# The hi/lo split of streamed weights, 1024 columns at a time instead of 512

## The chip, the cores and the metric

One core of one Trainium2 chip. The metric is the device time of one execution in microseconds (us); the kernel before was executed three times for it. A further execution was recorded by the hardware profiler, and all rows below come from that one.

## The reference, cut to what matters

Two small networks of float32 run one after the other on 512 tokens of width 1024.

```python
def first_block(x, ...):                     # DEPTH = 2
    for layer in range(2):
        h = rms_norm(x, norm_mix[layer])
        if layer < 1:
            x = x + short_conv_mixer(h, a_w_in, a_conv_w, a_w_out)
        else:
            x = x + nsa_mixer(h, b_w_qg, b_w_o, shared, rel_bias)   # three attention branches
        x = x + squared_relu_mlp(rms_norm(x, norm_mlp[layer]), mlp_w1[layer], mlp_w2[layer])
        if layer == 0:
            shared = nsa_shared_kv(rms_norm(x, kv_norm), w_kv, ...)  # with compress_blocks (phi)
    return rms_norm(x, final_norm)
# then, with 16 meta tokens set in front: mixer_block (z, xbc, dt, q, k, v and two gates from one
# product u @ w_in; an SSD scan in blocks of 128, a sliding-window attention with a sink, merged and
# projected), conv_ffn (d_ff 2816), a last norm
```

Nearly all the arithmetic is `activations @ weights`. Each weight is used once, for all 512 or 528 tokens, so the kernel streams 362 blocks ("chunks") of 128 x 1024 float32 weights, 512 KB each, in the order of their use.

## The kernel before, in words

**Three products for one.** The result has to be as exact as float32, and TensorE is fed with a rounded float32 type, `fp32r`. So each weight `w` is split: `whi` is `w` rounded to `fp32r` (a copy on ScalarE, ACT, line 161), `wlo = w - whi` (a subtraction, line 163, on VectorE, DVE, or on GpSimd, POOL). The activations have the same two parts, `hh` and `hl`, and a product is three matmuls: high by high, high by low, low by high.

**The stream.** `Stream` owns the weights. A chunk comes by one DMA on SyncE's queue (SP) into a tile `w32` of 1024 columns, of which there are two. It is split in two halves of 512 columns, into `whi` and `wlo`, of which there are four each, so four halves. A half holds four slots of 128 columns; `take` hands out the next slot, or two of them. At the first slot of a half `pre(half)` runs: it issues DMAs up to chunk `half // 2 + 1` and splits up to half `half + 2`. Half h goes into the buffers that half h - 4 had, so its split waits until TensorE (PE) has done the last matmul on that one. Halves are numbered 0 to 723, chunks 0 to 361; half h belongs to chunk h // 2. With `begin`, the first chunk is loaded in two pieces.

**Which engine subtracts.** `lo_mod` decides: a half with `ns % 4 < lo_mod` goes to POOL, the others to DVE. It is LO1 = 2 in the `nsa` stage (halves of every second chunk), LO2 = 4 in the window attention and the SSD stage (all halves), 0 elsewhere.

**Scaled splits.** Halves 192 to 209 and 226 to 249 are weights that are multiplied by a norm's gain while they are split. They are in the table `plan`; each is split in two or four pieces by pairs of instructions, ACT in line 157 and DVE in line 158, both with a scale.

**The order.** The kernel is written with the Tile framework, which orders each engine's instructions when the kernel is built, on a clock of its own: of those that it holds to be ready, the earlier in the program goes first. On the chip each engine then runs its own list in order, and a waiting instruction holds those behind it. All the weight DMAs are on SP's list, beside SP's loads of biases and its spills.

**The stages, in order of time.** `layer_a` (a convolution mixer); from about 90 to 143 us 48 DMAs on POOL's queue also write the skewed bias tables (`biases`). Then `mlp` 0, dense: matmul upon matmul of 512 columns. `nsa`: `kvraw` makes raw keys and values `kr`; `ebuild(s)` adds position terms to them, 32 additions `e` of which DVE runs 24 in a row (line 676); `kvsteps(0)` makes the first keys and values from scaled weights, its second half of the weights being chunk 104 (halves 208 and 209); `phi(s)` multiplies 8 chunks in all by `e`, two slots at a time, between steps of the attention; `br_a` and `br_b` are attention steps whose minima (of negated scores) and exponentials run on DVE (line 844) and ACT (line 846). `mlp` 1. Then the second network: `swa` (window attention; `head` has lines 1173 to 1224, and between the heads `xbc` and `gate_unit` run, with lines 1277 and 1283), `ssd` (the scan), `merge`, `ffn`, `tail`. In `swa` and `ssd` products are made by `gemm2`, which takes the 8 slots of a whole chunk first and then goes over them twice, once for each half of the 528 tokens.

`mm` in the rows is line 257, through which all matmuls go; line 266 is the low part of `split`, which splits activations.

Of the kernel before, what the change touches and what calls it, by code (L numbers as in the profile page):

```python
# [10 lines left out]
F32 = mybir.dt.float32  # L11
F32R = mybir.dt.float32r
I32 = mybir.dt.int32
AF = mybir.ActivationFunctionType
ALU = mybir.AluOpType
# [4 lines left out]
P = 128  # L20
# [23 lines left out]
BK = (2, 2, 2, 2)  # L44
PB = 10
PPB = 9


def _bucket(d):
# [73 lines left out]
class Stream:  # L123
# [9 lines left out]
    def begin(self, cols):  # L133
        c0, c1 = cols
        if c0 == 0:
            self.w32[self.nd] = self.pool.tile([P, 1024], F32, tag="w32", name="w32", bufs=2)
            self.nd += 1
        self.b.nc.sync.dma_start(self.w32[self.nd - 1][:, c0:c1], self.src[self.nd - 1][:, c0:c1])

    def pre(self, half):  # L140
        b, nc = self.b, self.b.nc
        while self.nd < min(self.nch, half // 2 + 2):
            t = self.pool.tile([P, 1024], F32, tag="w32", name="w32", bufs=2)
            nc.sync.dma_start(t, self.src[self.nd])
            self.w32[self.nd] = t
            self.nd += 1
        while self.ns < min(2 * self.nch, half + 3):
            c, o = divmod(self.ns, 2)
            src = self.w32[c][:, o * 512:o * 512 + 512]
            h = self.pool.tile([P, 512], F32R, tag="whi", name="whi", bufs=4)  # L150
            l = self.pool.tile([P, 512], F32R, tag="wlo", name="wlo", bufs=4)
            if self.ns in self.plan:
                g, ks = self.plan[self.ns]
                n = 512 // len(ks)
                for i, k in enumerate(ks):
                    a, sc = slice(i * n, i * n + n), b.pv(g, k)
                    nc.scalar.activation(out=h[:, a], in_=src[:, a], func=AF.Copy, scale=sc)
                    nc.vector.scalar_tensor_tensor(out=l[:, a], in0=src[:, a], scalar=sc, in1=h[:, a].bitcast(F32),  # L158
                                                   op0=ALU.mult, op1=ALU.subtract)
            else:  # L160
                nc.scalar.activation(out=h, in_=src, func=AF.Copy)  # L161
                eng = nc.gpsimd if self.ns % 4 < self.lo_mod else nc.vector
                eng.tensor_tensor(out=l, in0=src, in1=h.bitcast(F32), op=ALU.subtract)  # L163
            self.hl[self.ns] = (h, l)
            if o:
                del self.w32[c]
            self.ns += 1

    def take(self, key, r0, c0, n=128, width=1, rows=128):
        half, j = divmod(self.pos, 4)  # L170
        if j == 0:
            self.pre(half)
            self.hl.pop(half - 1, None)
        assert j + width <= 4
        for w in range(width):
            self.order.append((key, r0, c0 if isinstance(c0, tuple) else c0 + 128 * w, n))
        self.pos += width
        h, l = self.hl[half]
        a = j * 128
        e = a + (n if width == 1 else 128 * width)  # L180
        return h[:, a:e], l[:, a:e]


class Builder:
# [391 lines left out]
    def nsa(self, c):  # L576
# [87 lines left out]
        def ebuild(s):  # L664
            for b in range(2):
                for jh in range(2):
# [5 lines left out]
                    for g in range(4):  # L672
                        rr = slice(64 * (g % 2), 64 * (g % 2) + 64)
                        src = raws[s][g // 2][rr, A].rearrange("p (n j q) -> p q j n", j=8, q=2)
                        for q in range(2):
# [4 lines left out]
                                op=ALU.add)  # L680
                    eh, el = til("pp", PPB, "eh", F32R), til("pp", PPB, "el", F32R)
                    self.split(eh, el, e)
# [176 lines left out]
        def br_b(h, b, dst):  # L859
# [5 lines left out]
            for kts in ((0,), (1,), (2, 3)):  # L865
# [3 lines left out]
                for kt in kts:  # L869
                    segs.append((kt, off))  # L870
                    for qb in range(kt, 4):
                        self.tr(pt[:, off:off + 128], dst[qb][:, kt * 128:kt * 128 + 128])
                        off += 128
                ph, pl = til("pp", PPB, "ph", F32R), til("pp", PPB, "pl", F32R)
                self.split(ph[:, 0:off], pl[:, 0:off], pt[:, 0:off])
# [953 lines left out]
```

## Time and profile before

| What | Value |
|---|---|
| median of 3 runs | 2491.11 us (2489.51 to 2494.75) |
| the profiled execution, first to last instruction (span) | 2492.6 us |
| PE (TensorE matmul), busy | 2399.2 us, 96% |
| DVE (VectorE), busy | 1621.5 us, 65% |
| ACT (ScalarE), busy | 1116.3 us, 45% |
| POOL (GpSimd), busy | 596.3 us, 24% |
| mean granted clock of TensorE | 0.983 of full speed |
| DMA, mean | 97 GB/s |

A share of busy time is a mean over stages that have different limits; the rows by stretch below are the better guide. PEld is TensorE's loading of weights, which lies beside its matmuls. In a row `out<-in` names the tiles written and read, with partitions x elements and type; `x` stands ahead of a count; behind the bar is the idle time of the engine just ahead of these instructions, and what ended it. [...]

### The profile page before, as it was taken

How to read it: one execution, taken by the hardware profiler on the slowest of the kernel's cores; microseconds unless marked ns; L12 is line 12 of the kernel's file. 1: busy time of each engine (PE TensorE's matmuls, PEld its weight loads, DVE VectorE, ACT ScalarE, POOL GpSimd, SP SyncE). 2: the span in 40 equal slices, each digit the busy share in tenths (PEclk: the TensorE clock that was granted, in tenths of full speed). 3: DMA queues.
4: the chain of work that ended last, by engine and by line, in shares of the span. 5: the costliest groups of instructions: out<-in, count | busy, mean ns of one | idle time of the engine just before them, and what ended most of it. 6: DMA issues, size and time to landing. Idle time of an engine off the chain costs nothing.

```text
span 2492.6 us, 37785 instructions
## 1 busy us (share of the span) xinstructions
PE 2399.2 (96%) x14273; PEld 2090.8 (84%) x14273; DVE 1621.5 (65%) x3220; ACT 1116.3 (45%) x2252; POOL 596.3 (24%) x597
## 2 busy tenths in 40 slices
PE   8999999998899989999999989998999999999997
PEld 6778888886787768888888889988889999998996
DVE  6456525548888776435458894688987565874774
ACT  4233323333777663223435765555555433442442
POOL 1210000002434430000135445466656201000001
PEclk9999999999999999999999999999999999999998
DMA  4763333332421332322333222321212452333222
GB/s 144 175 155 92 97 93 93 102 117 83 130 86 51 103 93 93 94 93 93 95 99 108 67 75 90 94 65 52 64 52 85 145 188 91 95 90 95 90 93 77
DMA packets 87219, 242.68 MB, mean 97 GB/s; under 512 B 15435, under 2 KB 21835, under 8 KB 86987
## 3 DMA queue, kind: packets, MB, share of 16 engines
q1 hardware_dynamic: 82768, 228.96, 29.6%
q0 software_dynamic: 3136, 10.04, 2.0%
q8 instruction: 112, 1.84, 0.3%
q10 hardware_dynamic: 1132, 1.26, 0.2%
q14 instruction: 71, 0.58, 0.1%
HBM read 223.18 MB, written 24.51 MB: 99 GB/s over the span
## 4 chain that ended last, share of the span: by engine, by line
PE 82%; DVE 12%; ACT 2%; issue 2%; DMA 1%; SPq 0%; POOL 0%; DVEq 0%; ACTq 0%; POOLq 0%
PE mm L257 71%; PE o L257 3%; PE g L257 3%; PE s L257 2%; DVE cvt L1283 2%; PE pt L261 1%; DMA w<-in_ws_dram 1%; DVE pl L266 1%; PE u L257 1%; PE u L261 1%; DVE pp L1173 1%; PE st L257 0%; ACT ph L265 0%; DVE e L676 0%; DVE q L1109 0%
## 5 line engine op out<-in xcount | busy, mean ns | idle before, releaser
L257 PE MATMUL mm<-hh,whi 128*128 128x258 f32 (+2 forms) x2464 | 801.4, 326 | 25.5 <-ACT hh L305 6.9
L257 PE MATMUL mm<-hh,wlo 128*128 128x258 f32 (+2 forms) x2464 | 801.8, 326 | 6.4 <-DVE wlo L158 6.4
L257 PE MATMUL mm<-hl,whi 128*128 128x258 f32 (+2 forms) x2464 | 800.2, 325 | 2.6 <-DVE hl L306 2.6
L161 ACT ACTIVATE whi<-w 128x512 fp32r<-128x512 f32 x682 | 427.7, 630 | 814.9 <-PE mm L257 656.7
L163 DVE TENSOR_TENSOR wlo<-w,whi 128x512 fp32r<-128x512 f32 x516 | 362.5, 704 | 336.8 <-ACT whi L161 323.2
L257 PEld LDWEIGHTS mm<-hh,whi 128*128 128x128 f32 x2464 | 467.2, 190 | 71.6 <-ACT hh L305 9.8
L257 PEld LDWEIGHTS mm<-hh,wlo 128*128 128x128 f32 x2464 | 468.0, 190 | 50.1 <-DVE wlo L158 6.8
L257 PEld LDWEIGHTS mm<-hl,whi 128*128 128x128 f32 x2464 | 468.0, 190 | 46.3 <-issue 4.5
L163 POOL TENSOR_TENSOR wlo<-w,whi 128x512 fp32r<-128x512 f32 x166 | 232.7, 1408 | 209.1 <-ACT whi L161 179.9
L257 PE MATMUL mm<-b,whi 128*128 128x512 f32 (+1 forms) x699 | 273.5, 391 | 0.0
L257 PE MATMUL mm<-a,wlo 128*128 128x512 f32 (+1 forms) x699 | 273.5, 391 | 0.0
L257 PE MATMUL mm<-a,whi 128*128 128x512 f32 (+1 forms) x699 | 273.0, 391 | 0.0
L257 PEld LDWEIGHTS mm<-a,wlo 128*128 128x128 f32 x699 | 131.7, 188 | 29.9
L257 PEld LDWEIGHTS mm<-b,whi 128*128 128x128 f32 x699 | 131.7, 188 | 29.8
L257 PEld LDWEIGHTS mm<-a,whi 128*128 128x128 f32 x699 | 131.7, 188 | 29.7
L257 PE MATMUL mm<-oh,whi 128*128 128x258 f32 (+1 forms) x400 | 123.1, 309 | 2.8 <-ACT oh L265 2.1
L257 PE MATMUL mm<-ol,whi 128*128 128x258 f32 (+1 forms) x400 | 123.5, 309 | 0.0
L257 PE MATMUL mm<-oh,wlo 128*128 128x258 f32 (+1 forms) x400 | 123.5, 309 | 0.0
L291 POOL TENSOR_TENSOR acc<-sq 128x512 f32<-128x512 f32 (+1 forms) x5 | 7.0, 1397 | 438.1 <-ACT sq L286 438.1
L533 DVE TENSOR_TENSOR u<-mm,rstd 128x512 f32<-128x512 f32 x64 | 44.2, 691 | 88.6 <-PE mm L257 84.0
L996 POOL TENSOR_TENSOR sq<-sq 128x512 f32<-128x512 f32 x6 | 8.1, 1346 | 336.5 <-ACT sq L990 336.5
L257 PEld LDWEIGHTS mm<-oh,whi 128*128 128x128 f32 x400 | 76.7, 192 | 9.0 <-ACT oh L265 2.7
(535 smaller groups left out, 4260.2 us busy)
## 6 DMA issues: line engine op xcount, KB each, us to landing
w<-in_ws_dram SPq DMA_DIRECT2D x361, 512.0 KB, 3.5
sk<-line POOLq DMA_DIRECT2D x16, 320.0 KB, 10.5
bias<-sk SPq DMA_DIRECT2D x16, 256.0 KB, 2.9
sk<-line POOLq DMA_DIRECT2D x16, 192.0 KB, 10.0
x<-xs SPq DMA_DIRECT2D x8, 264.0 KB, 3.0
tatt<-gu SPq DMA_DIRECT2D x8, 258.0 KB, 2.3
matt<-yat SPq DMA_DIRECT2D x8, 258.0 KB, 2.0
yacc<-ya SPq DMA_DIRECT2D x8, 258.0 KB, 2.0
```

Source lines behind the costliest of these rows:

```text
L161: nc.scalar.activation(out=h, in_=src, func=AF.Copy)
L163: eng.tensor_tensor(out=l, in0=src, in1=h.bitcast(F32), op=ALU.subtract)
L257: self.nc.tensor.matmul(out, l, r, start=start, stop=stop)
L261: self.nc.tensor.transpose(out, in_, self.ident[0:n, 0:n])
L266: (eng or nc.vector).tensor_tensor(out=lo, in0=src, in1=hi.bitcast(F32), op=ALU.subtract)
L291: (nc.vector if k >= 6 else nc.gpsimd).tensor_tensor(out=na[:, c0:c1], in0=acc[:, c0:c1], in1=sq[:, c0:c1], op=ALU.add)
L533: nc.vector.tensor_tensor(out=u[:, XS], in0=p, in1=r[:, XS], op=ALU.mult)
L996: eng.tensor_tensor(out=a1[:, XS], in0=a1[:, XS], in1=s1[:, XS], op=ALU.add)
L1173: nc.vector.tensor_tensor_reduce(out=pp[:, b, 0:n], in0=s[:, 0:n], in1=bb, scale=1.0, scalar=nsink[:, h:h + 1], op0=ALU.add, op1=ALU.min, ...
L1283: nc.vector.scalar_tensor_tensor(out=t[:, s:W], in0=u[:, 0:W - s], scalar=hw(k), in1=t[:, s:W], op0=ALU.mult, op1=ALU.add)
```

## The change

A chunk is now split as a whole. `whi` and `wlo` are tiles of 1024 columns, two of each (WS = 2) in place of four of 512, so they take the same room. One ACT copy and one subtraction do the 1024 columns. Chunk 0 and the chunks with halves in `plan` are still split in halves or pieces, with the same instructions as before, into the large tiles. `pre` runs once per chunk: at the first slot of chunk `ch` it issues DMAs up to chunk `ch + 2` and splits up to chunk `ch + 1`. Chunk c takes the buffers of chunk c - 2. `lo_mod` goes by the number of the chunk: a chunk goes to POOL as a whole or not at all, as before, for both values in use.

```diff
--- before.py
+++ after.py
@@ -44,6 +44,8 @@
 BK = (2, 2, 2, 2)
 PB = 10
 PPB = 9
+WD = 2
+WS = 2
 
 
 def _bucket(d):
@@ -133,49 +135,53 @@
     def begin(self, cols):
         c0, c1 = cols
         if c0 == 0:
-            self.w32[self.nd] = self.pool.tile([P, 1024], F32, tag="w32", name="w32", bufs=2)
+            self.w32[self.nd] = self.pool.tile([P, 1024], F32, tag="w32", name="w32", bufs=WD)
             self.nd += 1
         self.b.nc.sync.dma_start(self.w32[self.nd - 1][:, c0:c1], self.src[self.nd - 1][:, c0:c1])
 
-    def pre(self, half):
+    def pre(self, ch):
         b, nc = self.b, self.b.nc
-        while self.nd < min(self.nch, half // 2 + 2):
-            t = self.pool.tile([P, 1024], F32, tag="w32", name="w32", bufs=2)
+        while self.nd < min(self.nch, ch + WD + 1):
+            t = self.pool.tile([P, 1024], F32, tag="w32", name="w32", bufs=WD)
             nc.sync.dma_start(t, self.src[self.nd])
             self.w32[self.nd] = t
             self.nd += 1
-        while self.ns < min(2 * self.nch, half + 3):
-            c, o = divmod(self.ns, 2)
-            src = self.w32[c][:, o * 512:o * 512 + 512]
-            h = self.pool.tile([P, 512], F32R, tag="whi", name="whi", bufs=4)
-            l = self.pool.tile([P, 512], F32R, tag="wlo", name="wlo", bufs=4)
-            if self.ns in self.plan:
-                g, ks = self.plan[self.ns]
-                n = 512 // len(ks)
-                for i, k in enumerate(ks):
-                    a, sc = slice(i * n, i * n + n), b.pv(g, k)
-                    nc.scalar.activation(out=h[:, a], in_=src[:, a], func=AF.Copy, scale=sc)
-                    nc.vector.scalar_tensor_tensor(out=l[:, a], in0=src[:, a], scalar=sc, in1=h[:, a].bitcast(F32),
-                                                   op0=ALU.mult, op1=ALU.subtract)
+        while self.ns < min(self.nch, ch + WS):
+            c = self.ns
+            src = self.w32.pop(c)
+            h = self.pool.tile([P, 1024], F32R, tag="whi", name="whi", bufs=WS)
+            l = self.pool.tile([P, 1024], F32R, tag="wlo", name="wlo", bufs=WS)
+            halves = [(2 * c + o, slice(o * 512, o * 512 + 512)) for o in range(2)]
+            if c == 0 or any(i in self.plan for i, _ in halves):
+                for i, hs in halves:
+                    if i in self.plan:
+                        g, ks = self.plan[i]
+                        n = 512 // len(ks)
+                        for j, k in enumerate(ks):
+                            a, sc = slice(hs.start + j * n, hs.start + j * n + n), b.pv(g, k)
+                            nc.scalar.activation(out=h[:, a], in_=src[:, a], func=AF.Copy, scale=sc)
+                            nc.vector.scalar_tensor_tensor(out=l[:, a], in0=src[:, a], scalar=sc, in1=h[:, a].bitcast(F32),
+                                                           op0=ALU.mult, op1=ALU.subtract)
+                    else:
+                        nc.scalar.activation(out=h[:, hs], in_=src[:, hs], func=AF.Copy)
+                        nc.vector.tensor_tensor(out=l[:, hs], in0=src[:, hs], in1=h[:, hs].bitcast(F32), op=ALU.subtract)
             else:
                 nc.scalar.activation(out=h, in_=src, func=AF.Copy)
-                eng = nc.gpsimd if self.ns % 4 < self.lo_mod else nc.vector
+                eng = nc.gpsimd if 2 * c % 4 < self.lo_mod else nc.vector
                 eng.tensor_tensor(out=l, in0=src, in1=h.bitcast(F32), op=ALU.subtract)
-            self.hl[self.ns] = (h, l)
-            if o:
-                del self.w32[c]
+            self.hl[c] = (h, l)
             self.ns += 1
 
     def take(self, key, r0, c0, n=128, width=1, rows=128):
-        half, j = divmod(self.pos, 4)
+        ch, j = divmod(self.pos, 8)
         if j == 0:
-            self.pre(half)
-            self.hl.pop(half - 1, None)
-        assert j + width <= 4
+            self.pre(ch)
+            self.hl.pop(ch - 1, None)
+        assert j + width <= 8
         for w in range(width):
             self.order.append((key, r0, c0 if isinstance(c0, tuple) else c0 + 128 * w, n))
         self.pos += width
-        h, l = self.hl[half]
+        h, l = self.hl[ch]
         a = j * 128
         e = a + (n if width == 1 else 128 * width)
         return h[:, a:e], l[:, a:e]
```

## Rows read from the trace of the kernel before

**Rows 1.** The chain that ended last: shares of the span by engine.
```profile
PE 82%; DVE 12%; ACT 2%; issue 2%; DMA 1%; SPq 0%; POOL 0%; DVEq 0%; ACTq 0%; POOLq 0%
```

**Rows 2.** Busy time by stretch: stretch, length, PE PEld DVE ACT POOL, PEclk, DMA share, GB/s.
```profile
300.00:400.00 100.00, 100.00 (x432) 81.09 (x431) 33.44 (x50) 24.02 (x38) 0.00 (x0) 1.00 0.31 95
1330.00:1500.00 170.00, 153.97 (x1207) 146.06 (x1207) 149.79 (x371) 114.24 (x300) 78.43 (x84) 0.98 0.26 74
1680.00:1900.00 220.00, 205.14 (x1466) 188.83 (x1465) 189.97 (x336) 118.28 (x251) 133.39 (x92) 0.95 0.20 62
600.00:660.00 60.00, 47.10 (x251) 38.64 (x249) 50.42 (x119) 34.93 (x86) 26.83 (x38) 0.89 0.41 126
```

**Rows 3.** The chain of 1330 to 1500 us, then of 1680 to 1900 us, by line.
```profile
by line: DVE cvt L1283 9.3%; DVE pp L1173 8.9%; issue 8.1%; PE mm L257 7.8%; DVE pl L266 6.2%; DVE q L1109 4.2%; PE g L257 4.1%; DVE pm L1186 4.0%; DVE tm L1184 3.5%; DVE of L1224 3.5%; PE u L261 3.3%; ACT pp L1176 3.1%; PE s L257 2.7%; DVE
by line: PE mm L257 43.9%; DVE cvt L1283 10.8%; PE u L257 4.4%; PE o L257 4.4%; DVE Ml L266 3.7%; DVE xs L1542 3.2%; PE s L257 2.6%; PE u L261 2.5%; DVE u L1277 2.0%; DVE cl L266 1.6%; ACT L L1490 1.5%; DVE dl L360 1.5%; DVE y L1503 1.4%; i
```

**Rows 4.** What PE waits for: us in all, times, longest us.
```profile
PE mm L257 <- DVE wlo L158: 6.4, 1, 6.4
...
PE mm L257 <- ACT whi L161: 5.2, 3, 3.8
```

**Rows 5.** Groups of the page: count, busy us, mean ns, idle before and its releaser.
```profile
L161 ACT ACTIVATE whi<-w 128x512 fp32r<-128x512 f32 x682 | 427.7, 630 | 814.9 <-PE mm L257 656.7
L163 DVE TENSOR_TENSOR wlo<-w,whi 128x512 fp32r<-128x512 f32 x516 | 362.5, 704 | 336.8 <-ACT whi L161 323.2
...
L163 POOL TENSOR_TENSOR wlo<-w,whi 128x512 fp32r<-128x512 f32 x166 | 232.7, 1408 | 209.1 <-ACT whi L161 179.9
```

**Rows 6.** Groups of instructions by form, whole span: lengths of different widths.
```profile
L1190 POOL TENSOR_TENSOR pp<-pp,rc 128x768 f32<-128x768 f32 x16 | 23.6, 1475 | 0.0
L846 ACT ACTIVATE pa<-pa,mn 128x512 f32<-128x512 f32 x32 | 23.0, 719 | 12.2 <-DVE mn L844 11.9
L844 DVE CUSTOM_DVE_ANT_0 pa<-s,bias 128x512 f32<-128x512 f32 x32 | 21.9, 685 | 0.5 <-DMA bias<-sk 0.5
L846 ACT ACTIVATE pc<-pc,mn 128x256 f32<-128x256 f32 x32 | 16.1, 503 | 2.1 <-DVE mn L844 1.8
L844 DVE CUSTOM_DVE_ANT_0 pc<-s,bias 128x256 f32<-128x256 f32 x32 | 13.4, 418 | 5.1 <-PE s L257 4.9
...
L1188 POOL TENSOR_TENSOR pp<-pp,rc 128x128 f32<-128x128 f32 x16 | 6.5, 409 | 45.4 <-DVE rc L1181 33.9 <-ACT of L1223 7.4 <-DVE ms L372 4.2
```

**Rows 7.** Timeline of POOL, then of DVE, 1424 to 1430 us: start, us, instruction.
```profile
1425.63 1.28 POOL L163 TENSOR_TENSOR wlo<-w,whi 128x512 fp32r<-128x512 f32 x1
...
1425.67 1.80 DVE L1283 SCALAR_TENSOR_TENSOR cvt<-u,hw,cvt 128x527 f32<-128x527 f32 x1
...
1427.87 0.75 DVE L1283 SCALAR_TENSOR_TENSOR cvt<-u,hw,cvt 128x526 f32<-128x526 f32 x1
```

**Rows 8.** Timeline of ACT, 108 to 150 us; in brackets idle before, and its releaser.
```profile
140.32 1.15 ACT L161 ACTIVATE whi<-w 128x512 fp32r<-128x512 f32 x2 [8.76 <-DMA w<-in_ws_dram]
```

**Rows 9.** Timeline of DVE, 588 to 640 us.
```profile
607.61 0.88 DVE L158 SCALAR_TENSOR_TENSOR wlo<-w,pkt,whi 128x256 fp32r<-128x256 f32 x2
...
609.60 10.05 DVE L676 TENSOR_TENSOR e<-kr,pkt 64x128 f32<-64x128 f32 x24
...
619.68 0.88 DVE L158 SCALAR_TENSOR_TENSOR wlo<-w,pkt,whi 128x256 fp32r<-128x256 f32 x2
```

**Rows 10.** Timeline of PE, 612 to 625 us.
```profile
613.43 0.40 PE L257 MATMUL mm<-hl,whi 128*128 128x512 f32 x1
...
621.25 0.63 PE L257 MATMUL mm<-hh,whi 128*128 128x512 f32 x1
```

**Rows 11.** Timeline of PE, 634 to 640 us.
```profile
637.03 0.39 PE L257 MATMUL mm<-wlo,eh 128*128 128x256 f32 x1 [0.86 <-POOL wlo L163]
```

**Rows 12.** Groups of POOL, 1330 to 1500 us, then 1680 to 1900 us.
```profile
L163 POOL TENSOR_TENSOR wlo<-w,whi 128x512 fp32r<-128x512 f32 x33 | 43.8, 1336 | 27.7 <-ACT whi L161 20.0 <-ACT ph L265 5.2 <-PE s L257 2.3
L163 POOL TENSOR_TENSOR wlo<-w,whi 128x512 fp32r<-128x512 f32 x47 | 69.9, 1494 | 56.2 <-ACT whi L161 43.1 <-DVE cvt L1283 6.0 <-DVE y L1503 3.7
```

## The prediction

> **What bounds the kernel now.** I read the chain of waits first: PE holds 82% of it, DVE 12%, ACT 2% [rows 1]. Then the busy time by stretch [rows 2]: in the dense stages PE is busy 100 of 100 us and issues 432 matmuls, one per 0.2315 us, so nothing a split does there can shorten the time; it can only add, by coming too late. In the window attention (1330 to 1500 us) PE idles 16.0 of 170 us and DVE is busy 149.8; in the SSD stage (1680 to 1900 us) PE idles 14.9 of 220 us and DVE is busy 190.0. There DVE leads: the DVE lines that the chain of those stretches names add up to 39.6% and 24.2% of it [rows 3]. Last, the list of what PE waits for: 6.4 us in one piece for a low part of line 158 and 5.2 us for high parts [rows 4]. So I price the change by stage: does a split of 1024 columns still arrive, and what does it hold up while it runs?
>
> **How many, and how long.** The 682 copies of line 161 [rows 5] become 2 + 340 (chunk 0 stays in halves), the 516 DVE subtractions 2 + 257, the 166 POOL subtractions 83; the 88 scaled pairs of lines 157 and 158 stay. No instruction of 1024 columns is in the trace. On ACT 256 more columns cost 0.719 - 0.503 = 0.216 us [rows 6], so 1024 take 0.630 + 0.432 = 1.06 us (bounds: 0.63 and 1.26, twice a half). On DVE 0.685 - 0.418 = 0.267 us per 256 gives 0.704 + 0.534 = 1.24 us (0.70 to 1.41). On POOL 640 columns more cost 1.475 - 0.409 = 1.07 us [rows 6], which would make 1.41 + 0.85 = 2.26 us; twice a mean half is 2.82, and twice a half that meets nobody (1.28, [rows 7]) 2.56. I take 2.4. So a chunk saves ACT 0.20 us, DVE 0.17 us, POOL about 0.2 us of busy time.
>
> **Dense stages: nothing.** A half-split starts when PE leaves its buffer (of the 814.9 us that ACT is idle ahead of its copies, PE ends 656.7, [rows 5]) and is used three halves later. [...] The DMAs of w32 keep two buffers and wait for the same split as before; issued one chunk earlier in SP's program, they are moved past SP's bias loads and spills, at 0.
>
> **Bias skew, 90 to 143 us.** Here the weight DMAs are late; ACT splits the moment they land (8.76 us idle for the DMA before 140.32, [rows 8]). PE can now start on such a chunk only when all 1024 high columns are copied: 1.06 - 0.63 = 0.43 us later, and its first low part 0.43 + 0.53 = 0.96 us later. The lateness does not add up from chunk to chunk, since the DMAs set the pace. I take +0.8 us (0 to 2).
>
> **The queue of ebuild, 604 to 628 us.** Chunk 104 holds halves 208 and 209, the second half of the kvsteps(0) weights, both scaled splits. In the trace half 208's two subtractions ran at 607.61, before ebuild(1); half 209's stood behind 24 additions of 10.05 us and ran at 619.68 [rows 9]. [...] Half 208 got ahead because its buffer came free half a chunk before the raw keys were ready. After, chunk 104 waits for PE to leave all of chunk 102, which is the moment at which kr of ebuild(1) becomes ready too; among ready instructions the earlier in the program goes first, so all four subtractions now stand behind the 24 additions. PE then stops 12 matmuls earlier (2.8 us), resumes some 0.9 us earlier, as 208's subtractions no longer precede the additions, and has 20 matmuls left instead of 8. [...] I take +3.0. [...]
>
> **phi, 625 to 656 us.** Eight chunks are eaten between attention steps. PE already waited 0.86 us for a POOL half [rows 11]; the whole chunk's low part comes 2.4 - 1.28 + 0.43 = 1.5 us later. Most of it lies beside waits for the attention's minima. I take +0.8 us (0 to 3).
>
> **Port, 1330 to 1960 us.** All low parts are on POOL here. At 1425.63 POOL began a low part of 1.28 us; DVE's line 1283 began at 1425.67 and took 1.80 us, where the same line took 0.75 us at 1427.87 [rows 7]: DVE stood still until POOL had ended. So what counts is how long one POOL instruction holds DVE's queue. Before it meets the hold DVE works on for x us, and loses hold - x. With two halves, some microseconds apart, a chunk costs 2(1.28 - x), with one instruction 2.4 - x. The difference is x - 0.16. At x = 0 the change gains 0.16 us a chunk; at x = 1.28 (half-holds lost nothing) it costs 1.1. With DVE's operations 0.4 to 0.75 us long I take x = 0.6: +0.44 us a chunk. The two stretches have 33 and 47 halves [rows 12], 16.5 and 23.5 chunks, so 7.3 and 10.3 us of DVE time; of that I put one half and three tenths on the path [rows 3]: 3.6 + 3.1 = +6.7 us. The bounds become -2.5 and +17 us.
>
> [...]
>
> **What the savings give back.** 340 x 0.20 us of ACT and 257 x 0.17 us of DVE are mostly beside a busy PE; on the path the splits stand with 5.2 us of PE's waits [rows 4], most of it the DMA's. I take -1.0 us (0 to -5).
>
> **Sum.** 0 + 0.8 + 3.0 + 0.8 + 6.7 - 1.0 = +10.3 us. The profiled execution spans 2492.6 us, 1.5 over the median of the runs, 2491.11, and inside their 2489.5 to 2494.8; it would become 2502.9. On the median that is 2501.4 us, 0.41% slower.
>
> **Rivals.** (1) Not slower: the order of DVE's queue at 604 us turns the other way. Place and price: the four subtractions of chunk 104 stand before the additions, PE's 6.4 us wait goes, -9 instead of +3.0, sum -1.7, 2489.4 us. For it: in the trace 208 did get ahead. Against it: 209 did not, and it had the same release that the whole chunk has now. It decides as soon as the planner sees the chunk's high part ready before kr. (2) The long hold costs nothing, because DVE loses as much to two holds as to one (x near 0.16), or its lost time falls beside PE's work: +3.6, 2494.7 us. For it: PE is still busy 91% and 93% of the two stretches [rows 2]. Against it: the 1.05 us lost in [rows 7]. (3) Slower still, through ACT: its queue is in order, and a copy that starts only when PE has left the whole chunk holds the exponentials behind it 0.43 us longer: 40 chunks x 0.43 = 17 us in the two stretches, half of it on the path, +8.6 on top, 2510.0 us. For it: ACT's exponentials are links of the attention's chain. Against it: ACT is idle a third of the first stretch and nearly half of the second.
>
> **Chances.** Forecast 0.45 (own range 2496.5 to 2505), rival one 0.16, two 0.23, three 0.16. A measurement of this kernel tells about 0.2% (5 us) from no change. Slower by more: the forecast and rival three but for their edges, 0.57. Within: rival two and a part of rival one, 0.27. Faster: the rest of rival one and what a new order of instructions may bring, 0.16. The range reaches from 2486 to 2512 us.
>
> **What would show it.** Dense stages: PE still 100 of 100 us with 432 matmuls. ebuild: the scaled subtractions of one chunk together, before or after the 24 additions; PE's wait near 8.3 us if after. Bias skew: PE's waits for high parts 1 us longer in total. Port: POOL instructions of 2.3 to 2.6 us, DVE operations of 2.5 us and more beside them, DVE's busy time in the two stretches up by some 17 us, and PE's idle time there up by 5 to 8. I am wrong if PE starves in a dense stage, if the POOL instruction is much under 2.3 us, or if DVE's busy time in the two stretches does not rise.

## The result, and the profile after

The changed kernel takes 2520.35 us (median of 4 runs, 2519.18 to 2523.21) where the kernel before took 2492.08 in the same comparison: ratio 1.0118, 95% interval 1.0102 to 1.0134, some 28 us slower. The direction was the one forecast; the size was not, +10.3 us, and the range ended at 2512. The profiled execution spans 2519.0 us, 26.4 more than that of before.

The first question is in which stage the time went. Counting the weight matmuls from the start gives the moment at which each kernel is done with a given chunk. Chunk 133, the end of the `nsa` stage, ends 1.8 us later than before (935.9 and 937.7), chunk 197 2.3 us later (1296.2 and 1298.5), and chunk 288, with which the window attention, the SSD stage and the first products after them are done, 26.0 us later (2052.3 and 2078.3). From there on nothing is added: chunk 361 is 26.0 us late too. So one stretch has 24 us of the 26, and it is the one in which POOL does all low parts.

Busy time by stretch of the kernel before, from the end of chunk 197 to that of chunk 288 (columns: stretch, length, PE, PEld, DVE, ACT, POOL with their instructions, granted clock, DMA share, GB/s):

```profile
1296.00:2052.00 756.00, 721.88 (x5537) 685.15 (x5537) 582.95 (x1176) 402.19 (x888) 364.81 (x296) 0.98 0.29 91
```

The same view of the changed kernel, a dense stage ahead of it:

```profile
300.00:400.00 100.00, 100.00 (x432) 81.09 (x431) 31.39 (x32) 20.18 (x20) 0.00 (x0) 1.00 0.31 95
1298.00:2078.00 780.00, 727.74 (x5540) 687.90 (x5539) 614.96 (x1160) 387.91 (x797) 338.18 (x223) 0.97 0.28 87
```

The dense stage is what it was [rows 2]: 100 of 100 us, 432 matmuls. In the other stretch ACT and POOL have less to do, as the merging intends, and DVE, which lost 16 instructions, is busy 32 us longer. PE's idle time goes from 34.1 to 52.3 us; the other 6 us of the 24 are PE itself, busy 727.7 instead of 721.9 us at a granted clock of 0.97 instead of 0.98 (PEclk in [rows 2], a share of full speed).

The chain of waits of the changed kernel (one row; before: [rows 1]), then the groups that answer to [rows 5]:

```profile
PE 74%; DVE 15%; ACT 4%; DMA 3%; issue 2%; POOL 1%; SPq 0%; DVEq 0%; ACTq 0%; POOLq 0%
...
L169 ACT ACTIVATE whi<-w 128x1024 fp32r<-128x1024 f32 x340 | 359.9, 1059 | 870.7 <-PE mm L263 614.4
...
L171 DVE TENSOR_TENSOR wlo<-w,whi 128x1024 fp32r<-128x1024 f32 x257 | 315.2, 1227 | 229.2 <-ACT whi L169 229.1
...
L171 POOL TENSOR_TENSOR wlo<-w,whi 128x1024 fp32r<-128x1024 f32 x83 | 205.5, 2476 | 214.5 <-ACT whi L169 206.6
```

PE's share of the chain falls from 82% to 74%, DVE's rises from 12% to 15%, ACT's from 2% to 4%, DMA's from 1% to 3% and POOL's from 0% to 1%. DMA's part has grown mostly by loads between 2030 and 2071 us, a place where the changed kernel falls back by only 1 us more. The instructions themselves are as long as estimated: ACT 1.059 us (1.06), DVE 1.227 (1.24), POOL 2.476 (2.4).

What such a POOL instruction does to DVE shows in one place; the timeline of POOL in the changed kernel, 1430 to 1434 us, and then that of DVE:

```profile
1430.38 2.38 POOL L171 TENSOR_TENSOR wlo<-w,whi 128x1024 fp32r<-128x1024 f32 x1 [0.46 <-ACT whi L169]
```

```profile
1430.41 2.43 DVE L1190 TENSOR_TENSOR tm<-pp,rc 128x64 f32<-128x64 f32 x1
1432.76 0.42 DVE L1283 TENSOR_TENSOR u<-mm,rstd 128x264 f32<-128x264 f32 x1
1433.10 0.75 DVE L1289 SCALAR_TENSOR_TENSOR cvt<-u,hw,cvt 128x526 f32<-128x526 f32 x1
```

A DVE operation on 64 columns began 0.03 us after POOL's and took 2.43 us; it ended 0.08 us after POOL's. The next one, another operation and four times as wide, took 0.42.

Last, what PE waits for, of the weights' parts (us in all, times, longest; before: [rows 4]):

```profile
PE mm L263 <- DVE wlo L163: 6.9, 1, 6.9
...
PE mm L263 <- ACT whi L169: 2.9, 3, 1.8
PE mm L263 <- DVE wlo L171: 2.4, 4, 0.9
...
PE mm L263 <- POOL wlo L171: 1.4, 1, 1.4
```

Beside the one wait of 6.9 us, which is outside the stretch (its place is in the section on the prediction), PE hardly ever waits for a split. The 24 us don't come from splits that are late for PE, at least not directly.

### The profile page after: what moved, and what is told of

It is laid out like the page before. It is cut to its first block, busy times and chain, and to the rows that moved or that the text cites. A ratio compares the mean times of both kernels' runs of the same rounds, so it can differ in the third digit from the quotient of the medians.

```text
span 2519.0 us, 36649 instructions
## 1 busy us (share of the span) xinstructions
PE 2405.5 (95%) x14273; PEld 2090.9 (83%) x14273; DVE 1618.8 (64%) x2963; ACT 1050.6 (42%) x1912; POOL 571.4 (23%) x514
## 4 chain that ended last, share of the span: by engine, by line
PE 74%; DVE 15%; ACT 4%; DMA 3%; issue 2%; POOL 1%; SPq 0%; DVEq 0%; ACTq 0%; POOLq 0%
PE mm L263 64%; PE o L263 3%; PE g L263 2%; DVE cvt L1289 2%; PE s L263 2%; DMA w<-in_ws_dram 2%; PE pt L267 1%; ACT whi L169 1%; DMA ma<-matt 1%; DVE e L682 1%; PE u L267 1%; DVE pl L272 1%; DVE z L1529 1%; PE u L263 1%; DVE Ml L272 1%
## 5 line engine op out<-in xcount | busy, mean ns | idle before, releaser
L169 ACT ACTIVATE whi<-w 128x1024 fp32r<-128x1024 f32 x340 | 359.9, 1059 | 870.7 <-PE mm L263 614.4
L171 DVE TENSOR_TENSOR wlo<-w,whi 128x1024 fp32r<-128x1024 f32 x257 | 315.2, 1227 | 229.2 <-ACT whi L169 229.1
L171 POOL TENSOR_TENSOR wlo<-w,whi 128x1024 fp32r<-128x1024 f32 x83 | 205.5, 2476 | 214.5 <-ACT whi L169 206.6
L552 DVE TENSOR_TENSOR x<-mm,x 128x512 f32<-128x512 f32 x32 | 22.1, 692 | 110.7 <-PE mm L263 110.7
```

Source lines behind the costliest of these rows:

```text
L552: nc.vector.tensor_tensor(out=x[:, XS], in0=p, in1=x[:, XS], op=ALU.add)
```

## The experiments

Two theories stood at first. **Hold**: while POOL's subtraction runs, a DVE operation beside it stands still to its end, so the length of one POOL instruction sets what DVE loses. **Lead**: with whole-chunk buffers a split may start only when PE has left a whole chunk, so everything behind it comes later. A third, **ACT**, says that the long copy holds ACT's queue. Each run was timed in three rounds against the kernel before on the same chip; ratios are to that.

**1. All instructions of 512 columns, chunk buffers kept.** Lead stays, merging goes.

```diff
-            if c == 0 or any(i in self.plan for i, _ in halves):
+            if True:
...
-                        nc.vector.tensor_tensor(out=l[:, hs], in0=src[:, hs], in1=h[:, hs].bitcast(F32), op=ALU.subtract)
+                        eng = nc.gpsimd if i % 4 < self.lo_mod else nc.vector
+                        eng.tensor_tensor(out=l[:, hs], in0=src[:, hs], in1=h[:, hs].bitcast(F32), op=ALU.subtract)
```

> The buffers and the lead stay as in the changed kernel (two of 1024 columns), but every copy and subtraction is of 512 columns again, as in the kernel before. Port (a long POOL instruction holds DVE): nearly all of the +28 us goes, 2492 to 2499 us, and DVE's busy time falls back. Lead (a split may start only when PE has left a whole chunk): nothing comes back, 2515 to 2521 us.

Measured 2493.43 us, 1.0004 (0.9993 to 1.0016): all of the loss is gone, and DVE is busy 579 us in the stretch instead of 615. The lead theory falls. The chunk buffers cost nothing that can be measured.

**2. Only POOL's subtraction in two of 512.**

```diff
-                eng.tensor_tensor(out=l, in0=src, in1=h.bitcast(F32), op=ALU.subtract)
+                n = 2 if eng is nc.gpsimd else 1
+                for i in range(n):
+                    a = slice(i * 1024 // n, (i + 1) * 1024 // n)
+                    eng.tensor_tensor(out=l[:, a], in0=src[:, a], in1=h[:, a].bitcast(F32), op=ALU.subtract)
```

> The changed kernel, with only POOL's subtractions cut in two of 512 columns; ACT and DVE keep theirs of 1024. Port: 2493 to 2502 us, DVE's busy time 25 to 40 us lower in 1298 to 1997 us. Lead: 2516 to 2521 us. Copies of 1024 columns on ACT as the cause: 2516 to 2521 us too.

Measured 2493.35 us, 1.0005 (0.9990 to 1.0020). DVE's busy time in the stretch falls by 24 us, just short of the 25 to 40 expected. So cutting the 83 POOL instructions of 2.5 us in two takes away the whole loss; the instructions merged on ACT and DVE cost nothing and bring nothing.

**3. Only ACT's copy in two of 512.**

```diff
-                nc.scalar.activation(out=h, in_=src, func=AF.Copy)
+                for i in range(2):
+                    a = slice(i * 512, i * 512 + 512)
+                    nc.scalar.activation(out=h[:, a], in_=src[:, a], func=AF.Copy)
```

> The changed kernel, with only ACT's copies cut in two of 512 columns; all subtractions stay at 1024. Port and lead: 2518 to 2523 us, as before the cut. ACT's queue held by the long copy: 2505 to 2512 us.

Measured 2517.62 us, 1.0105 (1.0090 to 1.0120): 3 us under the changed kernel, just under the range expected for no effect, and its interval overlaps that one's. The ACT theory falls. A new list of instructions by itself, which every such edit makes, did not bring the time back either.

**4. POOL's subtraction in four of 256** (as 2, with `n = 4`).

> The changed kernel, with POOL's subtractions cut in four of 256 columns. Port: a hold of some 0.65 us is hardly longer than DVE's own operation, so DVE loses less than with halves, and the time is below that of the kernel with halves on POOL by 5 to 25 us: 2470 to 2490 us. Lead: 2516 to 2522 us.

Measured 2479.28 us, 0.9952 (0.9934 to 0.9969): faster than the kernel before. Here is the stretch from chunk 197 to chunk 288 with POOL's pieces at 512 columns:

```profile
1295.00:2049.00 754.00, 720.65 (x5540) 681.81 (x5539) 590.90 (x1160) 388.71 (x797) 374.95 (x297) 0.99 0.28 90
```

and at 256:

```profile
1298.00:2035.00 737.00, 713.96 (x5532) 679.65 (x5532) 561.09 (x1153) 389.68 (x797) 414.47 (x445) 0.99 0.29 93
```

With pieces of 1024, 512 and 256 columns DVE is busy 615, 591 and 561 us with the same work, and the stretch takes 780, 754 and 737 us, although POOL is busy longer each time (338, 375, 414). One DVE line shows it by itself. `z<-th,z`, 16 operations of 516 columns, in the changed kernel (count, busy us, mean ns, idle before), then with pieces of 512, then of 256:

```profile
L1529 DVE SCALAR_TENSOR_TENSOR z<-th,z 128x516 f32<-128x516 f32 x16 | 27.5, 1716 | 10.2 <-ACT th L1528 10.2
```

```profile
L1532 DVE SCALAR_TENSOR_TENSOR z<-th,z 128x516 f32<-128x516 f32 x16 | 20.3, 1266 | 9.7 <-ACT th L1531 9.7
```

```profile
L1532 DVE SCALAR_TENSOR_TENSOR z<-th,z 128x516 f32<-128x516 f32 x16 | 14.0, 875 | 8.3 <-ACT th L1531 8.3
```

The same operation takes 1716, 1266 and 875 ns. In run 6 below, where POOL makes no low parts in this stage, it takes 791.

A long instruction could also cost time by holding up POOL's own next operation: in the chain of the changed kernel from 1406 to 1530 us POOL's splits hold 4.1% and POOL's line 1196 holds 3.9%. As the main cause this does not fit: with pieces of 256 columns a chunk keeps POOL busy longer, 3.5 us instead of 2.5, and the kernel is faster. A small share of it is not ruled out.

**5. Halves, but the second first.** Cutting POOL's work also brings the low part of the first slots sooner. To part that from the hold, the order of the halves is reversed.

```diff
-                for i in range(n):
+                for i in reversed(range(n)):
```

> POOL's subtractions in two of 512 columns, the second half of the chunk first, so that the low part of the first slots comes as late as with one instruction of 1024. Port: order within the chunk is nothing to DVE, 2490 to 2498 us, as with halves in order. Arrival (the first low part is late for PE): 2512 to 2521 us, as in the changed kernel.

Measured 2508.06 us, 1.0067 (1.0047 to 1.0087): neither. Both theories missed. The trace shows where the time went. In the stretch PE waits 0.4 us in all for low parts of weights; DVE is busy 603.6 us, where it is busy 590.9 with the halves in order (run 2):

```profile
1297.00:2064.00 767.00, 722.25 (x5542) 683.78 (x5541) 603.61 (x1167) 388.66 (x797) 371.63 (x297) 0.98 0.28 89
```

The stretch is 13 us longer and DVE is busy 13 us longer, with POOL instructions of the same length (1472 and 1477 ns). So most of the loss is again longer work of DVE and not a wait of PE for a late low part, and the length of POOL's instructions is not all that sets what DVE loses.

**6. No POOL in these stages** (`LO2 = 0` in the changed kernel: DVE subtracts, 1024 columns at a time).

> The changed kernel with LO2 = 0: in the window attention and the SSD stage DVE does the subtractions itself, 73 chunks of 1.23 us. Port: the 111 us that DVE's operations lie longer beside POOL's splits go, 90 us of own work come, so the time is a little below the changed kernel's, 2500 to 2516 us. If POOL's work were free for DVE: some 90 us more on a DVE that leads there, two thirds of it on the path, 2570 us or more.

Measured 2478.62 us, 0.9949 (0.9931 to 0.9966), 21 us below the range of the hold theory and far from that of free POOL work. DVE takes 74 subtractions more, 91 us at 1.227, and is busy less in the stretch than with POOL's help:

```profile
1298.00:2038.00 740.00, 716.91 (x5541) 683.26 (x5540) 589.98 (x1238) 390.38 (x797) 165.71 (x149) 0.98 0.29 92
```

590 us against 615. The expectation had DVE's balance nearly right (111 us gone, 90 added), but the stretch is shorter by 40 us where DVE's busy time falls by 25; why it gains more than DVE does was not traced.

**7. The kernel before, POOL's subtractions in two of 256** (the loop of 2, on tiles of 512 columns).

> The kernel before (tiles of 512 columns), with each of POOL's subtractions cut in two of 256 columns. Port: as much faster than the kernel before as the quarters made it with chunk tiles, 2475 to 2483 us; the merging on ACT and DVE itself is then worth nothing. If the gain of the quarters needs the chunk tiles: 2488 to 2494 us.

Measured 2468.83 us, 0.9907 (0.9887 to 0.9927), 6 us beyond the range of the first theory: the gain of short POOL instructions does not need chunk tiles. It is the fastest version found.

**8. POOL's subtraction in eight of 128** (as 2, with `n = 8`).

> Chunk tiles, POOL's subtractions cut in eight of 128 columns, some 0.4 us each by the 409 ns of another POOL operation of that width. Port: the hold is now shorter than most of DVE's operations, 2468 to 2480 us, at or below the quarters. If POOL itself becomes the limit (3.3 us a chunk instead of 2.5) or the number of holds counts as well: 2480 to 2495 us.

Measured 2488.40 us, 0.9991 (0.9981 to 1.0001). The first theory missed, the second was met: there is a bottom. The pieces took longer than I had taken from another line (the group in the same stretch):

```profile
L174 POOL TENSOR_TENSOR wlo<-w,whi 128x128 fp32r<-128x128 f32 x592 | 327.5, 586 | 90.8 <-ACT whi L169 88.5 <-ACT ct L1205 2.3
```

586 ns, not 409, and 327.5 / 74 = 4.4 us of POOL a chunk instead of 262.2 / 74 = 3.5 with quarters (their group stands in the last section) and 2.5 whole. DVE's busy time in the stretch is the lowest of all, 555.4 us, but the stretch is 6 us longer than with quarters. What ate the rest was not traced further; the last section shows what a piece costs.

**9 and 10. A hold without a consumer.** This is the sharpest test. On top of 6 (DVE makes the low parts), POOL does the same subtraction once more, in place in the weights' tile, and nobody reads it; in one instruction of 1024 columns (9) or four of 256 (10, shown). `b.idle` holds in the two stages only.

```diff
+                if b.idle:
+                    for i in range(4):
+                        a = slice(i * 256, i * 256 + 256)
+                        nc.gpsimd.tensor_tensor(out=src[:, a], in0=src[:, a], in1=h[:, a].bitcast(F32), op=ALU.subtract)
```

> As the kernel with the low parts on DVE (LO2 = 0), and behind each DVE subtraction of the two stages POOL subtracts the high part once more from the weights, in place, 1024 columns in one instruction; nobody reads the result (it is work added, and nothing waits for it but the next DMA into that tile, which has microseconds to spare). Port with an exclusive hold: DVE's operations get longer by some 1.5 us a chunk, as with the changed kernel's splits, 74 chunks, 80 to 110 us of DVE, and 2530 to 2570 us. Arrival alone (a POOL split matters only because its low part comes late): nothing waits for it, 2476 to 2484 us.

> The same unread work on POOL in four instructions of 256 columns. Port with an exclusive hold: 0.9 us a chunk, some 60 us of DVE, 15 to 40 us faster than with one of 1024 columns: 2510 to 2540 us. Port shared in proportion: not faster than with one of 1024, since POOL is busy longer in all. Arrival alone: 2476 to 2484 us.

Measured 2571.97 us, 1.0324 (1.0307 to 1.0342), and 2528.52 us, 1.0158 (1.0138 to 1.0177). Against 2478.62 without the unread work: +93 and +50 us. Run 9 is 2 us above its range, run 10 inside its own. The stretch and POOL's unread work with one instruction:

```profile
1300.00:2131.00 831.00, 748.58 (x5538) 702.81 (x5538) 711.68 (x1244) 387.48 (x797) 367.15 (x223) 0.94 0.26 83
...
L175 POOL TENSOR_TENSOR w<-w,whi 128x1024 f32<-128x1024 f32 x74 | 201.3, 2720 | 189.6 <-DVE wlo L171 123.8 <-issue 46.3 <-DVE yn L358 5.1
```

and with four:

```profile
1300.00:2091.00 791.00, 737.05 (x5540) 695.68 (x5539) 649.51 (x1242) 390.69 (x797) 433.94 (x445) 0.95 0.28 87
...
L175 POOL TENSOR_TENSOR w<-w,whi 128x256 f32<-128x256 f32 x296 | 273.2, 952 | 176.7 <-DVE wlo L171 101.5 <-issue 47.7 <-DVE ssum L1192 8.2
```

DVE does the same work in both and is busy 711.7 - 590.0 = 122 us longer with one long instruction a chunk, 649.5 - 590.0 = 60 us longer with four short ones: 1.64 and 0.80 us a chunk, where 1.5 and 0.9 had been expected. Nobody reads the result, and the trace has no wait of DVE for it: DVE's operations themselves take longer, which is the hold. The kernel's time is a less clean reading than DVE's, since the work also stands in POOL's list: ACT's copies wait for it 4.1 us in run 9 and 0.3 in run 10, and the chain of run 10 goes over it for 3.2% of the stretch, 25 us.

The traces also allow a count that leaves out DVE's own low parts. All versions share 1124 DVE operations of the stretch that make no low part of a weight (same line, tiles and shape, equally often). Their durations add up to 527 us in run 6, to 637 with the unread work in one piece and to 581 in four; with the low parts that are read it is 637 in the changed kernel and 582 in run 4 (599 in the kernel before, 614 in run 2). Who reads POOL's result makes no difference to DVE, the length of the instruction does. And it does not act in proportion to POOL's busy time, which is larger in the kernel that loses less (273.2 and 201.3 us).

**11 and 12. Two candidates.** The kernel before with `LO1 = LO2 = 0` (no low part on POOL), and with `LO2 = 2` (every second chunk on POOL) in pieces of 256 columns.

> The kernel before (tiles of 512 columns) with LO1 = LO2 = 0: no subtraction on POOL at all. Port: as the kernel with chunk tiles gained by LO2 = 0, 2472 to 2484 us, if the nsa stage does not mind. If POOL relieves DVE in tiles of 512 columns: 2500 us or more.

> The kernel before with LO2 = 2 (POOL has every second chunk of the two stages, DVE the others) and POOL's subtractions cut in two of 256 columns. Port: between the version with all on POOL in 256 columns (2468.8) and all on DVE, or below both if two half loads collide less: 2460 to 2475 us.

Measured 2478.87 us, 0.9959 (0.9944 to 0.9974), and 2471.96 us, 0.9932 (0.9917 to 0.9947). Both are inside their ranges. Each run of the mixture is faster than each run without POOL on the same chip; from all on POOL in pieces of 256 (7), timed on another chip, the interval of its ratio can't tell it apart.

**13. Quarters, the last first** (4 with the order of 5), for what run 5 had left open.

> Chunk tiles, POOL's subtractions in four of 256 columns, the last quarter of the chunk first, so that the first slots' low part comes some 2.7 us later than with quarters in order, and later than with one instruction of 1024. Hold alone: 2476 to 2484 us, as with quarters in order. A late first low part costs by itself, by its lateness (the reversed halves lost 15 us for some 1.5 us): 2495 to 2510 us. If the reversed halves lost only by another order of the instructions: no telling beforehand, but no growth with the lateness, 2476 to 2495 us.

Measured 2485.54 us, 0.9973 (0.9960 to 0.9986): some 6 us over quarters in order, with ratios whose intervals overlap, though by the lengths of the pieces (four of 0.9 us) the first slots' low part now comes later than in the changed kernel. It is above the 2476 to 2484 of the hold alone and inside the range without growth. So the price of run 5, 15 us for a smaller delay, is not a price of lateness that grows with it. Why the halves in reverse hold DVE longer stays open; the order of instructions that the edit happened to give is one candidate.

## Why the prediction was wrong

**Mechanism: right.** POOL's long instruction holds DVE, and the term I called "Port" is the loss. Runs 9 and 10 show it: for nearly the same unread work DVE was busy 122 us longer with one instruction a chunk and 60 us with four, and POOL was busy on that work 201.3 us with one and 273.2 with four. What in the chip makes DVE stand still no run shows; "Port" is a name for what was measured.

**The step that failed: "Port" priced 40 of 74 chunks and put the rest at nothing.** The heading of the step said 1330 to 1960 us, but I took only the 16.5 + 23.5 chunks of the two stretches that I had rows of. POOL has 74 chunks from chunk 197 to chunk 288, and nothing in the prediction says why the other 34 should be free. Comparing the moments at which the two kernels end the same weight matmul gives the price by place. The two stretches (1330 to 1500 and 1680 to 1900 us of the kernel before) became 3.0 and 4.3 us longer, 7.3 in all, against +6.7 forecast. The other 16.4 us of 23.7 came where I had priced nothing: 4.6 before 1330, 2.7 between the two, 9.1 after 1900.

**Inside the two stretches luck helped.** DVE was busy 0.7 and 11.9 us longer there, 12.6 against 17.6 forecast, and 19.4 us longer outside. So the price of +0.44 us a chunk is met only as a mean over the whole stretch, (614.96 - 582.95) / 74 = +0.43 us. The x = 0.6 behind it had been taken, not measured, and between runs 2 and 5 DVE's loss differs by 0.17 us a chunk at the same lengths. The share on the path, a half and three tenths by [rows 3], was too small in turn: 6.7 of 17.6 us forecast, 7.3 of 12.6 measured, 24 of 32 over the whole stretch. These shares are quotients of what was measured, and they change from place to place (after 1900 DVE is busy only 0.7 us longer and the time grows by 9.1), so how DVE's lost time reaches the end in each place stays open. The chain of before says what ended last when DVE still kept up in part of the stages; that its slack is used up when more comes on top is a reading that no run tests.

**The bounds** (-2.5 to +17) were built on the same 40 chunks, so the range was too narrow for the same reason, not by bad luck.

**Dense stages, 0:** right; 432 matmuls in 100 us, and from chunk 288 to 361 nothing was added. In the changed kernel a chunk's copy and subtraction took 2.32 us there (322.07 to 324.39) and the next copy, again released by PE, began 5.58 us after the first (327.65), so the split was done 3.3 us ahead.

**Bias skew, +0.8:** the changed kernel ended chunk 22 at 153.5 us, 1.2 us earlier. But the profiled executions of the other versions end it anywhere from 146.9 to 154.9 us, so this term is below what one profile can tell. PE's waits for high parts, forecast to grow by 1 us, fell from 5.2 to 2.9.

**ebuild, +3.0:** the mechanism came true by half, the price did not. Of the scaled subtractions of chunk 104 one got ahead of the 24 additions and three stood behind them (DVE's timeline):

```profile
609.51 0.47 DVE L163 SCALAR_TENSOR_TENSOR wlo<-w,pkt,whi 128x256 fp32r<-128x256 f32 x1
609.91 9.82 DVE L682 TENSOR_TENSOR e<-kr,pkt 64x128 f32<-64x128 f32 x24
619.76 1.28 DVE L163 SCALAR_TENSOR_TENSOR wlo<-w,pkt,whi 128x256 fp32r<-128x256 f32 x3
```

I had all four behind; before, two of them were ([rows 9]). PE's wait grew from 6.4 to 6.9 us instead of some 8.3, and the granted clock was back at 1.00 at 625 us, where before it stayed at 0.50 until 628. From 1.2 us ahead at chunk 22 the changed kernel went to 0.6 us behind at chunk 105, +1.8 in all; but it lost its lead at 590 to 595 us, ahead of the 24 additions, and from there to chunk 105 nothing was added. What cost the 2 us at 590 stays open. No run shows the +3.0: behind the 24 additions nothing was added, and at a granted clock of 0.50 the matmuls of 512 columns followed each other in 0.43 us (before, 621.25 to 622.95), 1.8 times the 0.2315 us at 1.00.

**phi, +0.8, and the savings, -1.0:** with the rest of `nsa`, from chunk 105 to chunk 133, the profiles differ by +1.2 us. No run has phi's term by itself, and between versions profiles differ by more than that there, so neither number is shown. Run 2, in which POOL's pieces are of 512 columns here too, gives the merging on ACT and DVE alone: 1.0005, so no saving that can be measured.

**Rivals.** Rival one, all four scaled subtractions ahead of the additions, did not happen; its -9 was an estimate, for which the trace of before has the wait of 6.4 us and, behind it, 8 matmuls of 512 columns at 0.43 us instead of 0.23. That two holds cost as much as one, and that DVE's lost time falls beside PE's work, is refuted by run 2. The ACT rival is refuted by run 3.

## What to carry to other kernels

Where POOL and DVE work side by side and DVE leads, as in these stages, price a POOL instruction by the time that it holds DVE. Here that went by its length (+110 us on DVE's operations with 74 instructions of 1024 columns, +55 with pieces of 256) and, less, by where it fell. Cut it: with pieces of 1024, 512, 256 and 128 columns (2.5, 1.5, 0.9 and 0.6 us) the kernel with chunk tiles took 1.0118, 1.0005, 0.9952 and 0.9991 of the time before. And price every chunk of every stage in which the two meet. Work moved to POOL to relieve DVE may cost DVE as much as doing it (here 615 us busy with POOL's help, 590 without). Merging instructions to save their overhead was worth nothing here on ACT and DVE (run 2), and cost 28 us on POOL, beside whose longer instructions DVE was busy 32 us longer.

## What the runs showed of the hardware that was not expected

POOL's pieces do not get shorter in proportion. A piece of 256 columns took 916 ns on average in run 4, where half of a 512-column piece in run 2 (1477 ns) would be 739. The group in the stretch, in pieces of 256:

```profile
L174 POOL TENSOR_TENSOR wlo<-w,whi 128x256 fp32r<-128x256 f32 x296 | 262.2, 916 | 132.7 <-ACT whi L169 132.5
```

Two things are in this, and the traces part them. Some of POOL's pieces have next to no DVE operation beside them (under 0.06 us of overlap). Their median is 457 ns at 128 columns (115 of 664 pieces, run 8), 737 at 256 (42 of 332, run 4), 1287 at 512 (8 of 166, run 2) and 2398 at 1024 (2 of 83, changed kernel). That is 275 to 280 ns for each 128 columns and, by subtraction, some 180 ns for each instruction. And beside DVE's operations POOL loses time as well: pieces of 256 that begin while a DVE operation runs take 973 ns on average (240 of the 332). At 128 columns the 180 ns stand eight times in a chunk, 1.4 of its 4.4 us, which is an end to the cutting if nothing else is.
